# Weight sums of seven block pairs a layer, made between attention and retention and kept in HBM

## The chip, the cores and the metric

The kernel runs on one NeuronCore of a Trainium2 chip. The core has a matrix engine (TensorE, in the profile PE for the matmuls and PEld for the loads of their stationary operand), a vector engine (VectorE, DVE), a scalar engine (ScalarE, ACT), a general engine (GpSimd, POOL) and a queue engine (SyncE, SP). Each takes its own instructions in a fixed order, and they wait for each other through semaphores. SBUF is the memory on the core, PSUM holds what the matmuls accumulate, in banks of 128x512 float32, and HBM is the large memory outside, reached by DMA. A DMA is issued by SP, ACT or POOL. The metric is the device time of one execution in microseconds (us).

## The reference, cut to what matters

Two layers of the same form work on 512 tokens of width 1024, in float32:

```python
h = rmsnorm(x, g_mix)
z = h @ w_in                      # attention q k v, retention q k v, retention gate, gate_a, gate_b
ya = sliding_window_sink_attention(aq, ak, av, sinks) @ w_a
r = chunkwise_retention(rq, rk, rv)              # four heads
r = r * rsqrt(mean(r * r) + EPS) * silu(rg)      # per head
yb = r @ w_b                                     # 1024 x 1024
mixed = sigmoid(ga) * ya + sigmoid(gb) * yb
x = x + mixed @ w_out                            # 1024 x 1024
h2 = rmsnorm(x, g_mlp)
x = x + square(relu(h2 @ w_up)) @ w_down         # 1024 x 4096 and 4096 x 1024
```

A last rmsnorm follows the second layer. What the change touches is the weights of `w_b`, `w_out` and `w_up`.

## The kernel before, in words

Activations lie transposed in SBUF, channels on the partitions and the 512 tokens along them. Weights come from HBM in units of 128x1024 float32 (512 KB), in the order that `unit_order` writes down. Every weight and every activation is kept as a high and a low part, and a product is made of three matmuls, high by high, high by low and low by high (`products`, lines 295 to 303).

A unit goes through three steps. `load_until` (line 183) issues its DMA on SP into one of three `raw` tiles (line 195). `split_until` (line 230) makes the high part on ACT (line 255) and the low part on DVE (line 256); each of `hi` and `lo` has three tiles, so that the split of a unit waits until PE is done with the unit three before, and the load waits until the low part of the unit three before has been made. Then PE uses the unit. A plain unit holds PE for 24 matmuls of 512 columns.

Some products are made two blocks of 128 outputs at a time with fewer multiplications, by the scheme of Strassen and Winograd: the inner dimension is halved, the two blocks are the other half, and seven products of halves take the place of eight. The kernel calls this a pair. It needs sums of activations, made by `sum_input` and used as "forms", and sums of weights. With one = unit j and two = unit j+1, each cut into LEFT and RIGHT of 512 columns, a pair consists of four parts (`add_part`, lines 217 to 229, four DVE additions of 128x512):

- part 0: one.LEFT, and s1 = two.RIGHT + two.LEFT (line 221)
- part 1: s1 - one.LEFT (line 224), and one.RIGHT
- part 2: one.LEFT - two.RIGHT (line 228), and the right side of part 1 less its left side (line 229)
- part 3: two.LEFT alone

`load_part` (line 205) loads a pair with three DMAs: one.LEFT and the whole of two for part 0 (lines 210 and 212; two is also the tile of part 3), and one.RIGHT for part 1 (line 215). Parts 1 and 2 are tiles of another pool, `big`, which has seven tiles of 128x1024 and serves gates, sums, tables and other short-lived things. A part is split as a plain unit is. In `narrow_pair` (from line 580) the matmuls have 256 columns, so that PE is through with a part after 24 short matmuls; `wide_pair` takes high by high and high by low in one matmul of 512 columns and low by high in one of 256 (lines 1259 and 1260). Between the matmuls ACT copies partial results from bank to bank (lines 595, 598, 602), and DVE adds the rest into the outputs.

Each layer has, in order: the attention's q, k and v and the attention; gate_a, the first retention heads and half of the retention's gate; retention q and k of head 1 (`qk(1)`), the retention's values of the first two heads (`values(0)`), `w_a`, the retention of heads 0 and 1 beside `qk(2)`, `qk(3)` and `values(1)`; the rest of the retention beside the other gates; two pairs of `w_b` and four plain units; two plain units of `w_out` and three pairs; four plain units of `w_up` and then fourteen pairs of it, with the units of `w_down` in between. In the first layer `qk(1)` to `values(1)` runs from about 140 to 240 us, the pairs of `w_b` from 311, those of `w_out` from 372, and the first two of `w_up` from about 424 us.

Which instruction stands where on an engine is decided by a scheduler of the language before the run (`schedule_with_timeline_sim=True`), from a model of the times; on the chip the order on each engine is fixed. POOL does next to nothing: it clears a tile and sets a few constants, and it issues no DMA.

Of the kernel before, what the change touches and what calls it, by code (L numbers as in the profile page):

```python
# [11 lines left out]
F32 = mybir.dt.float32  # L12
F32R = mybir.dt.float32r
AF = mybir.ActivationFunctionType
ALU = mybir.AluOpType
# [3 lines left out]
P = 128  # L19
T = 512  # L20
# [30 lines left out]
ASIDE = 48  # L51
FIRST_WIDE, LAST_WIDE = 6, 32
BETWEEN = (0, 2, 4, 5)
H = T // 2
CROSSED = (0, 1, 4, 5, 2, 3, 6, 7)


def unit_order():

    def plain(name, *at):  # L60
        return [(name, i) for i in range(*at)]

    def pairs(src, *firsts):
        return [("pair", j, part, src) for j in firsts for part in range(4)]

    order = plain("w_in", 26) + plain("w_a", 4) + plain("w_in", 26, 46)
    order += pairs("w_b", 0, 2) + plain("w_b", 4, 8)
    order += plain("w_out", 2) + pairs("w_out", 2, 4, 6)
    for what, q, i in mlp_sequence():
        if what == "first":  # L70
            order += plain("w_up", 4)
        elif what == "pair":
            order += pairs("w_up", 8 * q + 2 * i)
        elif what == "down":
            order += plain("w_down", 8 * q + 2 * i, 8 * q + 2 * i + 2)
        else:
            order += plain("w_down", 8 * q, 8 * q + 8)
    return order
# [13 lines left out]
def wide(chunk):  # L92

    return FIRST_WIDE <= chunk < LAST_WIDE
# [32 lines left out]
def decoder(ctx, tc, xT, x_first, w_in, w_a, w_b, w_out, w_up, w_down, tables, decay, band, triangles, g_last, out):  # L127
    nc = tc.nc
    weights = {"w_in": w_in, "w_a": w_a, "w_b": w_b, "w_out": w_out, "w_up": w_up, "w_down": w_down}
# [5 lines left out]
    dram = ctx.enter_context(tc.tile_pool(name="dram", bufs=1, space=bass.MemoryType.DRAM))  # L135
# [6 lines left out]
    def temp(name="t"):  # L142
        return tmp.tile([P, T], F32, tag="t", name=name)

    def big(name, dtype=F32):
        return tmp.tile([P, 2, T], dtype, tag="big", name=name, bufs=7)
# [18 lines left out]
    order = [(layer, *u) for layer in range(DEPTH) for u in unit_order()]  # L165
    raws, parts, homes = {}, {}, []
    state = {"next": 0, "loaded": 0, "split": 0}

    def halves(i):

        return (slice(0, UNIT // 2), slice(UNIT // 2, UNIT)) if i < 3 else (slice(0, UNIT),)
# [3 lines left out]
    def raw_tile():  # L175
        return wpool.tile([P, UNIT], F32, tag="raw", name="raw")
# [25 lines left out]

    LEFT, RIGHT = slice(0, UNIT // 2), slice(UNIT // 2, UNIT)

    def load_part(i):
        layer, _, j, part, src = order[i]
        one, two = (weights[src][layer, j + a] for a in range(2))
        if part == 0:
            raws[i] = raw_tile()
            nc.sync.dma_start(raws[i][:, LEFT], one[:, LEFT])  # L210
            raws[i + 3] = raw_tile()
            nc.sync.dma_start(raws[i + 3], two)
        elif part == 1:
            raws[i] = big("raw2").rearrange("p a t -> p (a t)")
            nc.sync.dma_start(raws[i][:, RIGHT], one[:, RIGHT])

    def add_part(i):
        part = order[i][3]
# [12 lines left out]
    def split_until(n):  # L231
        while state["split"] < min(n, len(order)):
            i = state["split"]
            load_until(i + 3)
            paired = order[i][1] == "pair"
            if paired:
                add_part(i)
            raw = raws[i]
            if homes and i >= len(order) - len(homes):
                home = homes[len(order) - 1 - i]  # L240
                hi, lo = (home[:, 2 * a : 2 * a + 2, :].rearrange("p a t -> p (a t)") for a in range(2))
            else:


                first = (ASIDE, ASIDE) if paired else (0, 0)
                if paired and order[i][4] == "w_up" and wide(order[i][2]):
                    first = (ASIDE, 0)
                hi, lo = (
                    wpool.tile([P, UNIT + P], F32R, tag=n, name=n)[:, a : a + UNIT] for n, a in zip(("hi", "lo"), first)
                )  # L250
            for at in (LEFT,) if paired and order[i][3] == 3 else halves(i):
                if i == 0 and at.start == 0:
                    nc.vector.tensor_copy(hi[:, at], raw[:, at])
                else:
                    nc.scalar.activation(hi[:, at], raw[:, at], AF.Copy)  # L255
                last_low[:] = [nc.vector.tensor_tensor(lo[:, at], raw[:, at], f32(hi[:, at]), ALU.subtract).ins]  # L256
            raws.pop(i - 3 if paired else i, None)
            parts[i] = (hi, lo)
            state["split"] += 1

# [110 lines left out]
    def all_of(steps):  # L371
        for step in steps:
            step()
# [85 lines left out]
    def end(layer, uT):  # L459
# [32 lines left out]

        H = T // 2
        steps = [(b, at) for b in range(NB) for at in ((slice(0, T),) if b < NB - 1 else (slice(0, H), slice(H, T)))]

# [40 lines left out]
    def layer_body(layer):  # L536
# [6 lines left out]
        def forms_home():  # L543

            t = slots.four()
            form = t[0].rearrange("p a (b t) -> p (a b) t", t=H).rearrange("p (j k s) t -> p j k s t", k=2, s=2)
            return t, form

        def sum_input(by_form, b, ks):

            (b11, b12), (b21, b22) = ((t[:, :, :H], t[:, :, H:]) for t in b)
            f = [big("sums").rearrange("p a (b t) -> p (a b) t", t=H) for _ in range(2)]
            t1, t2, t3, t4 = f[0][:, 0:2, :], f[0][:, 2:4, :], f[1][:, 0:2, :], f[1][:, 2:4, :]
# [24 lines left out]
        def block(half, tokens):  # L578
            at = slice(tokens * H, tokens * H + H)
            return [x_homes[k // 2][0][:, k % 2 :: 2, at] for k in range(4 * half, 4 * half + 4)]  # L580
# [307 lines left out]
        def qk(h, rate=1.0):  # L888
            chunk("w_in", layer, xs, put_ret(rk, h), rate)
            chunk("w_in", layer, xs, put_ret(rq, h), rate)  # L890
# [3 lines left out]
        def values(pair):  # L894

            banks = [bank(ps_mm, "rv") for _ in range(NB)]
            for u in range(4):
                hi, lo = unit("w_in", layer)
                for j in range(2):
                    k = 2 * u + j  # L900
                    cols = slice(j * T, (j + 1) * T)
                    for b, ps in enumerate(banks):
                        at = slice(b * P, (b + 1) * P)
                        products(
                            ps, [(tuple(m[:, at] for m in xs[k]), (hi[:, cols], lo[:, cols]))], k == 0, k == KD - 1
                        )
                    advance()
            for b, ps in enumerate(banks):
                hi, lo = slots.one(), slots.one()
                split(view(hi), view(lo), ps, rcol[:, b : b + 1])  # L910
                rv[pair, b] = (hi, lo)
# [16 lines left out]
        def silu(i):  # L928
            s = temp("sig")
            nc.scalar.activation(s, rg[i], AF.Sigmoid)  # L930
            nc.vector.tensor_tensor(rg[i], rg[i], s, ALU.mult)
# [95 lines left out]
        def retention(pair):  # L1027
            two = [Head(2 * pair), Head(2 * pair + 1)]
            for head in two:
                for js in ((0, 1), (2, 3)):  # L1030
                    head.scores(js)
                    yield
            two[0].outputs(0)
            yield
            two[0].outputs(1)
            yield
            two[1].outputs(0)
            yield
            yield
            two[0].norm()  # L1040
            yield
            two[1].outputs(1)
            yield
            yield
            yield
            two[1].norm()
            yield
            yield
            while 4 * pair + 3 not in rg:
                yield  # L1050
            for head in two:
                head.finish()
                yield
            for i in (pair, pair + 2):
                homes_r[i] = forms_home()
                by_form_r[i] = homes_r[i][1]
            sum_input(by_form_r, [rg_tiles[2 * pair], rg_tiles[2 * pair + 1]], 2 * pair)
# [8 lines left out]
        with tc.issue_after(last_exp[0]):  # L1066
            for hs in (slice(0, T // 2), slice(T // 2, T)):
                nc.scalar.activation(x[:, :, hs], x[:, :, hs], AF.Sigmoid)
            for i in range(4):
                silu(i)  # L1070
        qk(1)

        values(0)


        aT = [(a_h[:, c, :], a_l[:, c, :]) for c in range(4)]
# [12 lines left out]
            slots.give(*t[1])  # L1089

        background.append(retention(0))
        qk(2)
        qk(3)
        values(1)
        drain()
        background.append(retention(1))
# [218 lines left out]
        def pair(q, i, late):  # L1315
# [5 lines left out]
            def step(ins):  # L1321
                now = next(turn)
                while late and now == BETWEEN[4 - len(late)]:
                    with tc.issue_after(ins), tc.issue_after(last_low[0]):
# [237 lines left out]
```

## Time and profile before

| | |
|---|---|
| median of 3 runs | 1479.65 us (1479.59 to 1479.96) |
| the profiled execution | 1481.1 us |
| its span, first to last instruction | 1478.5 us |
| PE busy | 1467.9 us, 99% of the span |
| PEld busy | 1249.9 us, 85% |
| DVE busy | 1162.7 us, 79% |
| ACT busy | 810.3 us, 55% |
| POOL busy | 3.8 us |
| HBM | 153.80 MB read, 8.40 MB written |
| granted clock of PE | 0.999 |

The profiled execution is 2.6 us longer than its span, and 1.45 us longer than the median of the runs. Busy time of PE counts a matmul from its start until its result is complete. Matmuls overlap, so that a 128x512 matmul lasts 390 ns while the next one starts 227 ns later; PE can therefore be busy while a matmul starts late, and only the starts, or the waits, tell of that. In the rows of a group the words after the bar are busy time, the mean of one in ns, and the idle time of that engine just before them with what ended it. In the waits, the columns are the total, the number of times and the longest.

### The profile page before, as it was taken

The page shows a single profiled execution, that of the slowest core. Times are in us where ns is not written, and L with a number is a line of the kernel's source. Part 1 is how long each engine was busy: PE and PEld are TensorE (multiplying, and loading weights), DVE is VectorE, ACT ScalarE, POOL GpSimd, SP SyncE. Part 2 cuts the span into 40 slices and gives each one's busy share as a digit, 9 for nine tenths or more (in the row PEclk, how much of TensorE's full clock was granted, in tenths as well). Part 3 has the DMA queues.
Part 4 walks back from the last instruction along what each step waited for, and adds up shares of the span by engine and source line. Part 5 has one row for each costly group of instructions (what it writes and reads, how often), then busy time and mean ns, then how long its engine had stood idle before and what let it go on. Part 6 is the DMA issues. An engine that isn't in the chain of part 4 may idle for free.

```text
span 1478.5 us, 20008 instructions
## 1 busy us (share of the span) xinstructions
PE 1467.9 (99%) x7466; PEld 1249.9 (85%) x7466; DVE 1162.7 (79%) x1920; ACT 810.3 (55%) x1302; POOL 3.8 (0%) x14
## 2 busy tenths in 40 slices
PE   9999999999999999999999999999999999999998
PEld 7888888888988888888888888888889888888887
DVE  7998668778998787776678975686889977878763
ACT  7656356654674445444556743656547654444553
POOL 0000000000000000000000000000000000000000
PEclk9999999999999999999999999999999999999999
DMA  6422223246323333333543232323553323333241
GB/s 226 135 87 86 93 82 104 93 164 191 102 79 114 100 114 94 106 100 115 170 128 91 85 98 89 99 92 98 175 167 104 101 97 99 115 101 112 89 141 57
DMA packets 56945, 166.13 MB, mean 112 GB/s; under 512 B 6896, under 2 KB 7056, under 8 KB 56848
## 3 DMA queue, kind: packets, MB, share of 16 engines
q1 hardware_dynamic: 56560, 164.33, 34.9%
q8 instruction: 58, 0.95, 0.3%
q10 hardware_dynamic: 288, 0.52, 0.1%
q14 instruction: 39, 0.32, 0.1%
HBM read 153.80 MB, written 8.40 MB: 110 GB/s over the span
## 4 chain that ended last, share of the span: by engine, by line
PE 86%; DVE 6%; issue 6%; DMA 1%; ACT 0%; POOLq 0%; DVEq 0%; SPq 0%
PE mm L303 20%; PE mm L301 20%; PE mm L302 20%; PE mm L1259 10%; PE mm L1260 5%; DVE lo L256 2%; PE rv L301 2%; PE rv L302 2%; PE rv L303 2%; DVE r L309 1%; PE score L797 1%; PE r L301 1%; PE r L303 1%; PE r L302 1%; DMA inv<-row 0%
## 5 line engine op out<-in xcount | busy, mean ns | idle before, releaser
L302 PE MATMUL mm<-r,hi 128*128 128x512 f32 (+1 forms) x1568 | 572.7, 367 | 0.0
L301 PE MATMUL mm<-r,hi 128*128 128x512 f32 (+1 forms) x1568 | 570.6, 368 | 1.4 <-ACT eu L598 0.7
L303 PE MATMUL mm<-r,lo 128*128 128x512 f32 (+1 forms) x1568 | 563.1, 367 | 1.6 <-DVE lo L256 1.3
L255 ACT ACTIVATE hi<-raw 128x1024 fp32r<-128x1024 f32 (+1 forms) x334 | 334.4, 1003 | 393.1 <-PE mm L302 210.9
L256 DVE TENSOR_TENSOR lo<-raw,hi 128x512 fp32r<-128x512 f32 (+1 forms) x335 | 385.2, 1152 | 118.8 <-ACT hi L255 115.7
L303 PEld LDWEIGHTS mm<-r,lo 128*128 128x128 f32 x1568 | 293.3, 188 | 51.1 <-DVE lo L256 3.7
L301 PEld LDWEIGHTS mm<-r,hi 128*128 128x128 f32 x1568 | 294.0, 188 | 50.2 <-ACT eu L598 1.5
L302 PEld LDWEIGHTS mm<-r,hi 128*128 128x128 f32 x1568 | 294.3, 188 | 45.7
L1259 PE MATMUL mm<-r,hi 128*128 128x512 f32 x728 | 251.9, 391 | 0.0
L1260 PE MATMUL mm<-r,lo 128*128 128x256 f32 x728 | 200.4, 277 | 1.2 <-DVE lo L256 1.1
L1259 PEld LDWEIGHTS mm<-r,hi 128*128 128x128 f32 x728 | 136.5, 188 | 28.3
L1260 PEld LDWEIGHTS mm<-r,lo 128*128 128x128 f32 x728 | 136.6, 188 | 5.2 <-DVE lo L256 2.7
L1339 DVE TENSOR_TENSOR x<-x,mm 128x512 f32<-128x512 f32 x56 | 37.8, 687 | 29.2 <-PE mm L303 29.2
L1332 ACT ACTIVATE z<-z 128x512 f32<-128x512 f32 x56 | 32.5, 624 | 48.3 <-DVE z L1312 48.3
L302 PE MATMUL rv<-lo,r 128*128 128x512 f32 x128 | 49.8, 389 | 0.0
L303 PE MATMUL rv<-hi,r 128*128 128x512 f32 x128 | 49.5, 389 | 0.0
L301 PE MATMUL rv<-hi,r 128*128 128x512 f32 x128 | 49.4, 390 | 0.0
L308 ACT ACTIVATE r<-z 128x512 fp32r<-128x512 f32 x64 | 38.7, 621 | 12.6 <-DVE z L1022 12.5
L309 DVE TENSOR_TENSOR r<-z,r 128x512 fp32r<-128x512 f32 x64 | 43.1, 686 | 2.8 <-ACT r L308 2.6
L824 ACT ACTIVATE sm<-sm,st 128x256 f32<-128x256 f32 (+1 forms) x64 | 30.2, 474 | 19.1 <-DVE st L812 18.9
L1312 DVE SCALAR_TENSOR_TENSOR z<-z,rstd 128x512 f32<-128x512 f32 x52 | 35.7, 687 | 0.6
L221 DVE TENSOR_TENSOR raw<-raw 128x512 f32<-128x512 f32 x38 | 26.0, 684 | 7.0 <-DMA raw<-w_up_in 6.3
(261 smaller groups left out, 1693.0 us busy)
## 6 DMA issues: line engine op xcount, KB each, us to landing
raw<-w_in_in SPq DMA_DIRECT2D x89, 512.0 KB, 3.6
raw<-w_down_in SPq DMA_DIRECT2D x64, 512.0 KB, 3.6
raw<-w_up_in SPq DMA_DIRECT2D x36, 512.0 KB, 3.6
raw<-w_up_in SPq DMA_DIRECT2D x56, 256.0 KB, 2.8
raw<-w_b_in SPq DMA_DIRECT2D x12, 512.0 KB, 4.0
raw<-w_out_in SPq DMA_DIRECT2D x10, 512.0 KB, 7.1
raw<-w_a_in SPq DMA_DIRECT2D x8, 512.0 KB, 3.5
aside<-gb SPq DMA_DIRECT2D x8, 512.0 KB, 4.7
```

Source lines behind the costliest of these rows:

```text
L255: nc.scalar.activation(hi[:, at], raw[:, at], AF.Copy)
L256: last_low[:] = [nc.vector.tensor_tensor(lo[:, at], raw[:, at], f32(hi[:, at]), ALU.subtract).ins]
L301: nc.tensor.matmul(ps, ah, bh, start=start and i == 0, stop=False, **more)
L302: nc.tensor.matmul(ps, ah, bl, start=False, stop=False, **more)
L303: nc.tensor.matmul(ps, al, bh, start=False, stop=stop and i == n - 1, **more)
L308: nc.scalar.activation(hi, src, AF.Copy)
L309: nc.vector.tensor_tensor(lo, src, f32(hi), ALU.subtract)
L1259: nc.tensor.matmul(both, hi[:, c], m, start=start and k == 0, stop=False, **more)
L1260: nc.tensor.matmul(ps[:, :H], lo[:, c], m[:, 0, :], start=False, stop=k == 3 and start, **more)
L1312: nc.vector.scalar_tensor_tensor(z[:, :, at], z[:, :, at], 0.0, factor, ALU.max, ALU.mult)
L1332: nc.scalar.activation(z[:, i, :], z[:, i, :], AF.Square)
L1339: nc.vector.tensor_tensor(x[:, c, :], x[:, c, :], ps, ALU.add)
```

## The change

Seven of the pairs of each layer, those that begin at units 0 and 2 of `w_b`, 2, 4 and 6 of `w_out` and 4 and 6 of `w_up`, get their four weight sums earlier. A new function `sums_ahead` loads the two units into two tiles of `big` by two DMAs issued on POOL, makes the four sums on DVE (one in a tile of the pool `t`, three in place), and stores them by four DMAs of 128x512, issued on POOL too, into a tensor in HBM. The calls of `sums_ahead` stand around `qk(1)`, `values(0)`, `qk(2)` and `qk(3)`: one, one, two, one, one and the last one, in the order of `PARKED`. When such a pair comes up, `load_part` loads each side of each part by a DMA of its own on SP, 128x512, from the weights or from the stored sums: seven DMAs for the pair in place of three, with all four parts in `raw` tiles, where before two parts were. `add_part` is left out for it, and a part's `raw` tile is given back after its own split.

```diff
+PARKED = (("w_b", 0), ("w_b", 2), ("w_out", 2), ("w_out", 4), ("w_out", 6), ("w_up", 4), ("w_up", 6))
...
+    park = {at: dram.tile([P, 4, T], F32, name="park_%s_%d" % at) for at in PARKED}
+
+    def is_parked(i):
+        return order[i][1] == "pair" and (order[i][4], order[i][2]) in park
+
     def load_part(i):
         layer, _, j, part, src = order[i]
         one, two = (weights[src][layer, j + a] for a in range(2))
+        if is_parked(i):
+            sums = park[src, j]
+            raws[i] = raw_tile()
+            sides = ((one[:, LEFT], sums[:, 0, :]), (sums[:, 1, :], one[:, RIGHT]), (sums[:, 2, :], sums[:, 3, :]), (two[:, LEFT],))
+            for side, part_of in zip((LEFT, RIGHT), sides[part]):
+                nc.sync.dma_start(raws[i][:, side], part_of)
+            return
         if part == 0:
...
+    def sums_ahead(layer, src, j):
+
+        w1, w2 = (big("ahead").rearrange("p a t -> p (a t)") for _ in range(2))
+        for a, w in enumerate((w1, w2)):
+            nc.gpsimd.dma_start(w, weights[src][layer, j + a])
+        s1 = temp("ahead1")
+        nc.vector.tensor_tensor(s1, w2[:, RIGHT], w2[:, LEFT], ALU.add)
+        nc.vector.tensor_tensor(w2[:, RIGHT], w1[:, LEFT], w2[:, RIGHT], ALU.subtract)
+        nc.vector.tensor_tensor(w1[:, LEFT], s1, w1[:, LEFT], ALU.subtract)
+        nc.vector.tensor_tensor(w1[:, RIGHT], w1[:, RIGHT], w1[:, LEFT], ALU.subtract)
+        for n, part in enumerate((s1, w1[:, LEFT], w2[:, RIGHT], w1[:, RIGHT])):
+            nc.gpsimd.dma_start(park[src, j][:, n, :], part)
...
-            if paired:
+            if paired and not is_parked(i):
                 add_part(i)
...
-            raws.pop(i - 3 if paired else i, None)
+            raws.pop(i - 3 if paired and not is_parked(i) else i, None)
...
+        to_park = [partial(sums_ahead, layer, *at) for at in PARKED]
+
+        def ahead(n):
+            all_of(to_park[:n])
+            del to_park[:n]
+
+        ahead(1)
         qk(1)
-
+        ahead(1)
         values(0)
+        ahead(2)
...
         background.append(retention(0))
+        ahead(1)
         qk(2)
+        ahead(1)
         qk(3)
+        ahead(9)
         values(1)
```

## The prediction

> **What bounds the kernel.** I read the page's first part, then the waits of the matrix engine, then stretches of time, then one stall in the timeline.
>
> ```profile
> span 1478.5 us, 20008 instructions
> PE 1467.9 (99%) x7466; PEld 1249.9 (85%) x7466; DVE 1162.7 (79%) x1920; ACT 810.3 (55%) x1302; POOL 3.8 (0%) x14
> ...
> PEld mm L303 <- DVE lo L256: 3.7, 6, 0.9
> PEld mm L1260 <- DVE lo L256: 2.7, 4, 0.8
> PEld mm L301 <- ACT eu L598: 1.5, 3, 0.6
> PEld mm L301 <- ACT eu L602: 0.9, 2, 0.5
> PEld mm L301 <- DVE gb L858: 0.3, 1, 0.3
> ```
>
> PE is the bound, and its number of matmuls isn't changed. All that the change can win is time in which PE waits. Those five rows are nearly all of it after the start: 3.7 + 2.7 + 1.5 + 0.9 + 0.3 = 9.1 us, of which 6.7 end with VectorE and 2.4 with ScalarE. The stretches show where (columns: the stretch and its length, busy time of PE, PEld, DVE, ACT and POOL with the number of instructions, clock, DMA share, GB/s):
>
> ```profile
> 140.00:190.00 50.00, 50.00 (x225) 41.54 (x224) 30.82 (x43) 20.73 (x29) 0.00 (x0) 1.00 0.31 100
> 190.00:230.00 40.00, 40.00 (x193) 33.88 (x192) 26.73 (x46) 23.55 (x38) 0.00 (x0) 1.00 0.30 87
> 311.00:345.00 34.00, 33.72 (x228) 30.77 (x227) 30.30 (x45) 19.25 (x28) 0.00 (x0) 1.00 0.63 202
> 345.00:372.00 27.00, 27.00 (x125) 22.47 (x124) 26.97 (x36) 12.69 (x16) 0.00 (x0) 1.00 0.60 195
> 372.00:404.00 32.00, 30.96 (x246) 29.77 (x245) 31.10 (x48) 21.17 (x35) 0.00 (x0) 1.00 0.30 90
> ...
> 431.00:450.00 19.00, 18.39 (x110) 15.63 (x109) 18.71 (x33) 13.73 (x22) 0.00 (x0) 1.00 0.36 113
> ```
>
> From 311 to 450 us DVE is busy 89 to 100%, and PE has its holes there, in the pairs of w_b, w_out and w_up. From 140 to 230 us DVE has 50 + 40 - 30.82 - 26.73 = 32.4 us to spare, and PE has no hole. One hole, in a w_out pair:
>
> ```profile
> 388.71 0.69 DVE raw L224
> 389.40 0.66 DVE r L312
> 390.06 0.33 DVE x L1199
> 390.39 0.60 DVE acc L395
> 390.99 1.15 DVE lo L256
> ...
> 391.23 0.28 PE L302 MATMUL mm<-r,hi 128*128 128x256 f32 x1
> 392.18 0.38 PE L303 MATMUL mm<-r,lo 128*128 128x256 f32 x1 [0.67 <-DVE lo L256]
> 392.40 0.28 PE L301 MATMUL mm<-r,hi 128*128 128x256 f32 x1
> ```
>
> The chain runs through DVE without a gap: a weight sum, work for the next norm, then the low part that PE waits for. PE starts these matmuls 0.12 us apart; here 0.95 passed, 0.83 too many.
>
> **The change, part by part.**
>
> *The sums leave the pairs.* Per pair four additions of 128x512:
>
> ```profile
> L221 DVE TENSOR_TENSOR raw<-raw x38: 627/692/694, 302.7 to 1406.7; 128x512 f32<-128x512 f32 x38
> ...
> L229 DVE TENSOR_TENSOR raw<-raw x38: 680/690/693, 321.3 to 1417.8; 128x512 f32<-128x512 f32 x38
> ...
> 328.48 0.68 DVE L228 TENSOR_TENSOR raw<-raw 128x512 f32<-128x512 f32 x1
> 329.08 0.69 DVE L229 TENSOR_TENSOR raw<-raw 128x512 f32<-128x512 f32 x1
> ```
>
> One lasts 0.69 us and the next starts 0.60 later, so a pair loses 4 x 0.60 = 2.4 us of DVE. The longest wait of PE for DVE is 0.9. In 311 to 345 us two pairs take 4.8 of 30.30 us off, in 372 to 404 three take 7.2 of 31.10, and the two of w_up give 4.8 before 450. The low parts come sooner by more than the waits, so I take 0.9 of the 6.7 us as won: 6.0. The upper bound is the whole 9.1, if ScalarE's copies come sooner too; the lower is 0, if what comes next is as late. Next in line are ScalarE's copies (line 598), for which PE waits until 378.1 us here:
>
> ```profile
> 376.56 0.71 ACT L311 ACTIVATE r<-x 128x512 fp32r<-128x512 f32 x1
> 377.17 0.61 ACT L394 ACTIVATE sq<-x 128x512 f32<-128x512 f32 x1
> 377.69 0.36 ACT L598 ACTIVATE eu<-mm 128x256 f32<-128x256 f32 x1
> ```
>
> ScalarE is held by work for the next norm, which no sum feeds. So the 2.4 us stay in the sum.
>
> *The sums come back earlier.* 7 x 2.4 = 16.8 us go into the 32.4 us that are free from 140 to 230 us; five pairs stand before about 190, where 12 us meet 19.2 free. By volume this costs nothing. By order it can: DVE takes instructions in turn, and a sum that waits for its load holds all behind it. The tightest place is the third pair. In the built order of DVE its first sum stands right after the low part that is made at 161.48 us, and ahead of the four instructions that empty the banks of the values:
>
> ```profile
> 161.48 1.23 DVE L256 TENSOR_TENSOR lo<-raw,hi 128x1024 fp32r<-128x1024 f32 x1 [2.85 <-ACT hi L255]
> 164.83 2.79 DVE L312 SCALAR_TENSOR_TENSOR r<-rv,rcol,r 128x512 fp32r<-128x512 f32 x4 [2.12 <-ACT r L311]
> ...
> 169.38 0.46 PE L301 MATMUL mm<-r,hi 128*128 128x512 f32 x1
> ...
> raw<-w_up_in SPq DMA_DIRECT2D x36, 512.0 KB, 3.6
> ...
> raw<-w_out_in SPq DMA_DIRECT2D x10, 512.0 KB, 7.1
> ...
> spill<-x SPq DMA_DIRECT2D x8, 256.0 KB, 2.0
> ```
>
> Its load reuses a tile of the first pair, and so waits on POOL for the first pair's last store. That sum ends about 155 us by the order, a store takes 2.0, a load 3.6, and POOL issues three more DMAs in between, for which I take an estimate of 1 us each, three times SP's 0.33. So the load is there at 155 + 1 + 2.0 + 2 + 3.6 = 163.6, against 162.7 when DVE comes to it. PE needs the first emptied bank at 169.38 less its 1 us of matmuls moved ahead: DVE can be late some 3 us. With 7.1 for the load, as in the DMA bursts, the 3.5 more just eat that. The traces show no DMA of POOL; between no cost and a late load at each of five pairs, I take 0.4 us a layer, nearer the free end because PE has three split units and a bank in hand.
>
> [...]
>
> *More loads on SP.* Seven DMAs in place of three a pair, at 0.33 us each to issue:
>
> ```profile
> raw<-w_up_in SPq DMA_DIRECT2D x56, 256.0 KB, 2.8
> ...
> raw<-w_out_in SPq DMA_DIRECT2D x12, 256.0 KB, 7.3
> ...
> L210 SPq DMA_DIRECT2D raw<-w_up_in x28: 327/328/328, 404.6 to 1399.6; - x28
> ...
> L256 DVE TENSOR_TENSOR lo<-raw,hi x335: 680/1221/1229, 6.0 to 1435.1; 128x1024 fp32r<-128x1024 f32 x127, 128x512 fp32r<-128x512 f32 x41
> L255 ACT ACTIVATE hi<-raw x334: 612/1062/1068, 6.9 to 1433.6; 128x1024 fp32r<-128x1024 f32 x164, 128x512 fp32r<-128x512 f32 x3
> ```
>
> 4 x 0.33 = 1.3 us more of SP a pair hide in the 9.9 us that PE takes for it (3.5 parts of 24 x 0.118, the pitch in the hole's rows). But the four parts now share three raw tiles, so a part's load waits for the low part of three parts before. The round is two issues 0.7, landing 2.8, high part 1.06, low part 1.22: 5.8 us, against 3 x 2.8 = 8.4 of PE. With the 7.3 of the burst it is 10.3 and 1.9 us late, of which a part's split can give back 2 x 2.8 - 2.3 = 3.3. That cover goes if DVE is still full, as from 345 to 372 us (26.97 of 27). Bounds 0 and 1.9 a layer; 0.35, since most of the burst lies before the pairs.
>
> *Traffic.* A layer adds 7 MB read and 7 MB written from 140 to 230 us, 163 GB/s on top of 87 to 100, and 5.5 MB in the pairs. PE loses 0.28 of 34 us through the 202 GB/s of 311 to 345 us, so I take it that only landings suffer; they are in the terms above. POOL's 42 issues a layer replace nothing, and only one clearing of a tile (late in the first layer) stands behind them.
>
> Sum against the profiled execution, 1481.1 us: -6.0 + 2 x 0.4 + 2 x 0.35 = -4.5, 1476.6. The median is 1.45 lower: 1475.2 us.
>
> **Rivals.**
>
> *DVE held by POOL's loads (slower).* Place: the first sum of the third to fifth pair, each with a load behind the stores of an earlier pair. If each of POOL's DMAs takes 3 us longer than assumed, a store and a load put the sum 6 us late; the bank's 3 us cover half, and 3 us of PE go per pair and layer: 3 x 3 x 2 = 18, less 6.0: +12, 1491.7. PE waits from 1.5 us a DMA on, and from 2 us the loss, 6 x (2 x 2 - 3) = 6, is more than the gain. For it: 163 on top of 100 GB/s is more than the 195 to 202 of the stretches where loads took 7 us. Against: PE has 50.00 of 50 us and 40.00 of 40 there, with slack that the trace doesn't use. [...]
>
> *The stalls change hands (no change).* DVE is early, but PE then waits for ScalarE's copies (2.4 us, kept) and for parts loaded late, 1.9 a layer: -6.0 + 3.8 + 0.8 = -1.4, 1478.2. For it: landings of 7 us in w_out. Against: the cover of 3.3 us.
>
> *All holes close.* -9.1, nothing lost: 1470.6. For it: ScalarE's copies often wait for tiles that DVE frees. Against: 378 us above.
>
> **How the numbers follow.** Forecast 0.52, all holes 0.06, change of hands 0.20, held DVE 0.22. Within 0.2% is 3.0 us either way, about what these runs can tell. Of the forecast's cases a tenth win less than 3.0: faster 0.53, same 0.25, slower 0.22. The likeliest case alone spans 1472.5 to 1477.5. The range leaves out a bit of the holes' end and the worse half of the held DVE: 1471 to 1486.
>
> **What would show it.** Right: lines 221 to 229 down from 38 to 24 each; DVE from 311 to 450 us lower by 16 us and higher by as much from 140 to 230; waits of the weight loads for line 256 below 1.5 us in total; no wait of PE from 140 to 270. Wrong: a DVE row of the new sums with several us of idle ended by a POOL DMA and PE waiting for line 312 or 1087 right after (held DVE); PE waiting for line 255 with a raw load as its last cause (change of hands).

## The result, and the profile after

| | before | after |
|---|---|---|
| median of the runs | 1479.62 us (4 runs, 1479.36 to 1479.96) | 1487.10 us (4 runs, 1485.48 to 1489.33) |
| the profiled execution | 1481.1 us | 1485.48 us, the fastest of the four |
| its span | 1478.5 us | 1483.7 us |

After over before is 1.0051, with a 95% interval of 1.0034 to 1.0069: 7.5 us slower, where 4.4 us faster was forecast. Lines 256, 301 to 303, 312, 595 and 598 of before are lines 282, 327 to 329, 338, 621 and 624 after; the four sums of a pair are now lines 247, 250, 254 and 255 where they stay in place, and 236 to 239 where they are made ahead. One execution of a kernel below, the five pairs with the copy first, took 1821 us at a clock of 0.75 and is left out of that kernel's ratio.

The page of the changed kernel begins with the busy time of each engine:

```profile
span 1483.7 us, 20353 instructions
...
PE 1468.5 (99%) x7466; PEld 1250.6 (84%) x7466; DVE 1162.6 (78%) x1920; ACT 810.1 (55%) x1302; POOL 49.4 (3%) x98
```

PE does the same work in nearly the same busy time, so the 5.2 us more of span are, for the most part, again time in which it waits or starts late. Counting the matmuls that start more than 0.15 us later than the usual pitch (0.227 us after a matmul of 512 columns, 0.118 after one of 256), PE lost 6.9 us before and 12.5 us after behind the start, in the two profiled runs. Its largest waits (total, times, longest):

```profile
PEld mm L327 <- ACT mm L621: 4.6, 3, 2.1
PEld mm L327 <- DVE r L338: 2.0, 1, 2.0
PEld mm L329 <- DVE lo L282: 1.8, 3, 1.0
PEld mm L327 <- DVE gb L884: 1.7, 2, 1.3
```

The waits that the change aimed at did go: those for low parts were 3.7 + 2.7 us, and of the first 1.8 us are left, of the second (line 1297 now) 0.4. New ones took their place: 4.6 for the first copy of a pair (line 621), which was in no row of before, 2.0 for the evacuation of the values' banks, 1.7 for the gates. The stretches, with the columns as in the prediction:

```profile
140.00:190.00 50.00, 48.42 (x216) 39.92 (x215) 36.78 (x54) 18.77 (x25) 14.03 (x26) 1.00 0.80 267
190.00:230.00 40.00, 40.00 (x193) 33.93 (x192) 34.91 (x62) 23.95 (x40) 7.06 (x13) 1.00 0.62 212
...
311.00:345.00 34.00, 31.60 (x205) 28.70 (x204) 26.74 (x38) 18.32 (x28) 0.00 (x0) 0.95 0.58 196
345.00:372.00 27.00, 27.00 (x126) 22.56 (x126) 23.24 (x31) 11.95 (x15) 0.00 (x0) 1.00 0.67 232
372.00:404.00 32.00, 30.96 (x237) 29.66 (x236) 26.52 (x38) 20.93 (x33) 0.00 (x0) 1.00 0.46 140
404.00:431.00 27.00, 27.00 (x142) 23.24 (x142) 22.87 (x30) 20.27 (x28) 0.00 (x0) 1.00 0.46 142
431.00:450.00 19.00, 18.95 (x135) 17.29 (x134) 17.79 (x25) 15.53 (x27) 0.00 (x0) 1.00 0.44 141
```

DVE does what was meant: 15.8 us less from 311 to 450 us, 14.1 more from 140 to 230. PE loses 1.6 us before 190 and 2.4 from 311 to 345, where its clock is 0.95 besides. I take the places one by one.

**At 171 us, in the first layer.** The chain of waits, in order of time (start, us, what):

```profile
156.46 5.57 DMA park_w_b<-ahead
162.31 6.98 DMA ahead<-w_out_in
169.32 0.70 DVE ahead L236
170.65 0.75 DVE r L338
```

A store of an earlier pair, then the third pair's load, then its first sum, and only then the first evacuation, for which PE starts 1.7 us late. DVE stood idle for 5.9 us ahead of that sum, and PE's reserve took up the rest. That is the place that the prediction named, with slower transfers. In the second layer the same sum waits 6.0 us at 899 us, and no matmul starts late for it. Over all pairs (KB each, median us to landing):

```profile
ahead<-w_out_in POOLq DMA_DIRECT2D x12, 512.0 KB, 6.8
park_w_out<-ahead POOLq DMA_DIRECT2D x24, 256.0 KB, 4.4
...
ahead<-w_b_in POOLq DMA_DIRECT2D x8, 512.0 KB, 4.7
park_w_b<-ahead POOLq DMA_DIRECT2D x16, 256.0 KB, 5.6
```

**At 320 us, the first pair of w_b.** The chain of waits there:

```profile
309.73 0.96 DVE own L447
310.71 1.58 DMA row<-own
312.30 3.76 DMA inv<-row
316.08 1.29 DVE z L1047 x2
317.38 1.22 DVE z L1048 x2
320.56 0.78 PE mm L327
```

This is the norm of the last retention head. Its reciprocal starts at 309.73 us; before it started 7.9 us sooner, as the timeline of before shows:

```profile
301.86 0.95 DVE L421 RECIPROCAL own<-own 128x128 f32<-128x128 f32 x1 [3.05 <-ACT own L420]
...
310.04 1.24 ACT L308 ACTIVATE r<-z 128x512 fp32r<-128x512 f32 x2 [1.33 <-DVE z L1022]
...
320.30 0.37 ACT L595 ACTIVATE mm<-mm 128x256 f32<-128x256 f32 x1
```

The timeline after, at the same place:

```profile
318.01 1.23 ACT L334 ACTIVATE r<-z 128x512 fp32r<-128x512 f32 x2 [1.48 <-DVE z L1048]
319.27 0.37 ACT L621 ACTIVATE mm<-mm 128x256 f32<-128x256 f32 x1
...
319.69 0.39 PE L327 MATMUL mm<-r,hi 128*128 128x256 f32 x1 [1.91 <-ACT mm L621]
```

ScalarE's queue now holds the splits of the retention's output ahead of the pair's first copy; they wait for the norm, the copy waits behind them, and PE behind the copy. Before, the norm was through 8 us sooner, and no matmul waited for it. PE then gets slower for a while (stretch, as above):

```profile
321.00:324.00 3.00, 3.00 (x8) 2.33 (x8) 3.00 (x6) 2.99 (x5) 0.00 (x0) 0.50 0.56 186
324.00:328.00 4.00, 4.00 (x20) 3.29 (x20) 3.03 (x6) 1.93 (x4) 0.00 (x0) 1.00 1.01 340
```

For 3 us after the wait the granted clock is 0.50, which is 1.5 us lost on top. In the second layer the same norm is late by less: 1.3 us at 1053 us.

The second layer has one more loss at 1076 us, with another cause. A matmul starts 0.7 us late for a high part (line 281) and one 0.7 us late for the low part after it. The chain of waits leads back to the load of that unit of w_b:

```profile
1069.54 4.96 DMA raw<-w_b_in
```

It is issued when its raw tile comes free, as the low part of an earlier part has been made, and lands 5.0 us later. So here a load comes late.

**At 382 and 1115 us, the first pair of w_out.** From the timeline:

```profile
379.58 0.71 ACT L337 ACTIVATE r<-x 128x512 fp32r<-128x512 f32 x1
380.20 0.62 ACT L417 ACTIVATE acc<-x 128x512 f32<-128x512 f32 x1
380.72 0.71 ACT L337 ACTIVATE r<-x 128x512 fp32r<-128x512 f32 x1
381.33 0.62 ACT L420 ACTIVATE sq<-x 128x512 f32<-128x512 f32 x1
381.85 0.36 ACT L621 ACTIVATE mm<-mm 128x256 f32<-128x256 f32 x1
...
382.27 0.39 PE L327 MATMUL mm<-r,hi 128*128 128x256 f32 x1 [1.04 <-ACT mm L621]
```

Four instructions for the next norm stand ahead of the copy, and PE starts 1.2 us late, once in each layer. Before, the built order had the copy first (at 372.60 us) and the norm's work from 375.42 on.

**Why the norm is late** isn't told by any duration. A scheduler writes the order of each engine before the run. In the order that PE is given, the sum of squares of the last retention head stands behind 927 matmuls of the products in the first layer before, and behind 951 after; in the second layer behind 4176 and 4186. Its matmul in the first layer, before:

```profile
299.91 0.39 PE L416 MATMUL ssq<-sh,ones 128*128 128x512 f32 x1
```

and after:

```profile
307.79 0.39 PE L442 MATMUL ssq<-sh,ones 128*128 128x512 f32 x1
```

At 0.227 us each, 24 matmuls are 5.4 us and 10 are 2.3; with the 1.7 us lost at 171 us, that makes 7.1 of the 7.9 us. So my theory was: **the sums made ahead change the built order, the norm goes behind, and the first w_b pair waits for it** (theory A below). The rival, theory B: the parts are loaded late, with seven loads in place of three and four parts in three raw tiles.

### The profile page after: what moved, and what is told of

It is laid out like the page before. It is cut to its first block, busy times and chain, and to the rows that moved or that the text cites. A ratio compares the mean times of both kernels' runs of the same rounds, so it can differ in the third digit from the quotient of the medians.

```text
span 1483.7 us, 20353 instructions
## 1 busy us (share of the span) xinstructions
PE 1468.5 (99%) x7466; PEld 1250.6 (84%) x7466; DVE 1162.6 (78%) x1920; ACT 810.1 (55%) x1302; POOL 49.4 (3%) x98
## 4 chain that ended last, share of the span: by engine, by line
PE 89%; issue 5%; DMA 3%; DVE 2%; ACT 1%; POOL 0%; POOLq 0%; ACTq 0%; DVEq 0%; SPq 0%
PE mm L327 21%; PE mm L329 21%; PE mm L328 21%; PE mm L1296 10%; PE mm L1297 5%; PE rv L327 2%; PE rv L328 2%; PE rv L329 2%; PE score L823 1%; DMA raw<-w_b_in 1%; DMA park_w_b<-ahead 1%; PE r L327 1%; PE r L329 1%; PE r L328 1%; PE pT L778 0%
## 5 line engine op out<-in xcount | busy, mean ns | idle before, releaser
L334 ACT ACTIVATE r<-sums 128x1024 fp32r<-128x1024 f32 x24 | 25.3, 1055 | 8.4 <-DVE sums L586 4.3
```

The source lines that it names most:

```text
L334: nc.scalar.activation(hi, src, AF.Copy)
```

## The experiments

All were timed beside the kernel before, which took 1479.64 to 1480.05 us in those sets.

### One side of the change at a time

Loads and pairs as in the changed kernel, without the sums:

```diff
-        to_park = [partial(sums_ahead, layer, *at) for at in PARKED]
+        to_park = []
...
-            sides = ((one[:, LEFT], sums[:, 0, :]), (sums[:, 1, :], one[:, RIGHT]), (sums[:, 2, :], sums[:, 3, :]), (two[:, LEFT],))
+            sides = ((one[:, LEFT], two[:, RIGHT]), (two[:, LEFT], one[:, RIGHT]), (one[:, LEFT], two[:, RIGHT]), (two[:, LEFT],))
```

> The sums are not made at all and nothing is stored; in the place of each stored sum the pair loads an unsummed side of the weights of the same size, so the seven products of these pairs are computed from wrong sums, and the loads of a pair, seven of 128x512 on SP, and the work of PE, ACT and DVE inside the pairs are as in the changed kernel. Theory A (the part made ahead does the harm: it puts the last two retention heads' norm behind, 24 matmuls in the first layer and 10 in the second in the built order, and that norm holds the first w_b pair): the norm stands where it stood before, the waits of PE at the start of the w_b pairs (2.07 + 0.31 us and the slow matmuls after them, 1.28 us) and the 1.74 us at 171 are gone, the waits of DVE stay gone; what is left is at most the copies of ScalarE at the w_out pairs, 2 x 1.3. Time 1479.6 - 6.0 + 2.6 = 1476 us, between 1474 and 1479. Theory B (the parts are loaded late: seven loads for three, three raw tiles for four parts): everything is lost that the changed kernel lost after 310 us, 1487.1 - 1.8 = 1485 us.

Measured 1476.96 us, ratio 0.9981 (0.9972 to 0.9990). Its largest wait (line numbers are one less than in the changed kernel):

```profile
PEld mm L326 <- ACT mm L620: 2.5, 2, 1.2
```

Theory B falls as the cause of the 7.5 us: with all 49 loads a layer in place, the pairs are faster than before. Of the new waits the copy in w_out is left; one for a later copy (line 623 of this kernel), at 325 us, is 0.9 us long. The late load at 1076 us is gone too. It is seen in the six kernels that make sums of w_b ahead and use them, so it takes both sides; why is not shown.

The other side, sums made and stored but not used:

```diff
-        return order[i][1] == "pair" and (order[i][4], order[i][2]) in park
+        return False
```

> The sums are loaded, made and stored ahead as in the changed kernel, but the pairs load their weights and make their sums as before, and nothing reads the stored ones. Theory A: all the losses of the part made ahead without the gain: 1.8 us at the third pair's sum, and the late norm at the w_b pairs, 4.2 us in the first layer with the slow matmuls and 1.4 in the second: 1479.6 + 7.4 = 1487 us, more if the sums inside the pairs now meet the late norm. Theory B: only the 1.8 us: 1481.4 us.

Measured 1493.63 us, ratio 1.0095 (1.0080 to 1.0111). The loss is all on this side, and larger than expected. Among its waits are

```profile
PEld mm L329 <- DVE lo L282: 6.5, 8, 1.6
PEld mm L327 <- ACT r L334: 3.5, 2, 2.4
...
PEld mm L1297 <- DVE lo L282: 2.7, 4, 0.8
```

The sums in the pairs now meet the late norm on DVE: low parts cost 6.5 + 2.7 us where before they cost 6.4 (and the bank at 171 costs 3.0, and the granted clock is 0.59 from 172 to 176 us and 0.66 from 322 to 327). So the two sides are not additive: -2.7 and +14.0 alone, +7.5 together.

### Is it the amount of added work, or its place?

Five pairs, those of w_out and w_up, same calls in the same places (five fill the calls up to the one between `qk(2)` and `qk(3)`):

```diff
-PARKED = (("w_b", 0), ("w_b", 2), ("w_out", 2), ("w_out", 4), ("w_out", 6), ("w_up", 4), ("w_up", 6))
+PARKED = (("w_out", 2), ("w_out", 4), ("w_out", 6), ("w_up", 4), ("w_up", 6))
```

> Only the three pairs of w_out and the two of w_up are made ahead, in the order of the same calls; the two of w_b are made in place as before. In the built order the retention's norms stand where they stood before the change (after 855, 927, 4107 and 4176 matmuls of the products), and the third pair's first sum still stands ahead of the evacuations. Theory A: no late norm, so the w_b pairs start as before; the waits of DVE in the w_out and w_up pairs close, 2.3 us a layer; 1.8 us stay at the third pair's sum, and 2 x 1.3 at ScalarE's copies: 1479.6 - 4.6 + 1.8 + 2.6 = 1479.4 us, and 1477 if the copies' order comes back too. Theory B: five of the seven pairs still load late, 1479.6 + 5/7 of 7.5 = 1485 us.

Measured 1481.42 us (1478.0 to 1484.3), ratio 1.0008 (1.0000 to 1.0017). The profiled run, the fastest, has no wait for the norm, 1.9 us at 171 and 1.2 + 1.2 at the copies. So the places are as theory A has them, and its 1479.4 is 2 us low. Across its runs the granted clock goes from 1.000 at 1478.0 us to 0.997 at 1484.3; a thousandth over 1480 us is 1.5 us.

The last call moved one projection later:

```diff
-        ahead(9)
         values(1)
         drain()
         background.append(retention(1))
+        ahead(9)
```

> The sums of the last two of the seven pairs, those of w_up, are called after the values of heads 2 and 3 instead of before them. In the built order the last retention norm then stands behind 984 matmuls of the products in the first layer and 4233 in the second: 33 and 47 later than in the changed kernel, at 0.227 us each 7.5 and 10.7 us. Theory A: the first w_b pair waits by that much longer, less what PE can do in between: 1487 + 18 = 1505 us, and no less than 1492. Theory B: as the changed kernel, 1487 us.

The expectation speaks of the last two pairs; at that point one is left, so that this moves one pair's sums only. Measured 1510.16 us, ratio 1.0206 (1.0192 to 1.0220): 23 us more than the changed kernel. The largest wait:

```profile
PEld mm L327 <- ACT r L334: 15.3, 4, 6.3
```

Four additions, called one projection later, cost three times the 7.5 us of the whole change. The amount of work is the same, so it can't explain that. The norm's place goes with it: 33 and 47 matmuls later than in the changed kernel.

The opposite: that last call left out, and all else as in the changed kernel.

```diff
-PARKED = (("w_b", 0), ("w_b", 2), ("w_out", 2), ("w_out", 4), ("w_out", 6), ("w_up", 4), ("w_up", 6))
+PARKED = (("w_b", 0), ("w_b", 2), ("w_out", 2), ("w_out", 4), ("w_out", 6), ("w_up", 4))
```

> The changed kernel without its last call, the one between the last two projections and the values of heads 2 and 3: that call makes the sums of one pair only, the second of w_up (the earlier run that moved that call moved one pair, not two). The other six pairs are called where the changed kernel calls them, and the second w_up pair makes its sums in place. In the built order the norms then stand behind 859, 927, 4111 and 4181 matmuls in place of 883, 951, 4115 and 4186. If one call of 2.4 us of VectorE at that place costs through the order: the 4.2 us at the first w_b pair go, and part of the 1.4 and 1.7 in the second layer; the wait at 171, the copies of w_out stay, and 0.5 a layer comes back in the second w_up pair: 1487.1 - 4.2 - 1.5 + 1.0 = 1482.4 us. If the cost goes by the amount of work ahead: six sevenths of it stay, 1486 us.

Measured 1482.81 us, ratio 1.0021 (1.0012 to 1.0030), against 1482.4 expected by the order and 1486 by the amount. The wait at the first w_b pair of the first layer is gone. That the sum came out so well is in part luck. In the profiled run, which at 1485.91 us is the second slowest of eleven, the second w_up pair costs 2.1 us in each layer where 0.5 was expected (the reason stands below, under fewer pairs), and the wait at 171 us is 2.8 us.

Over the kernels run, the place of the last norm in the built order goes with the late starts at the first w_b pair (how much later than the usual pitch PE starts a matmul that waits for the first copy, for the splits of the retention's output or for the gates, in the profiled run of each; some have more than one such start):

| kernel | calls right before `values(1)` | layer 1: behind, late | layer 2: behind, late |
|---|---|---|---|
| before | none, no sums made ahead | 927, 0 | 4176, 0.2 us |
| sums left out (e1), five pairs (e3, e8) | none | 927, 0 | 4176, 0 |
| two pairs (e10) | none | 917, 0 | 4176, 0 |
| three pairs (e9) | none | 917, 0 | 4181, 1.3 |
| four pairs (e12) | none | 927, 0 | 4181, 1.5 |
| six pairs (e11) | none | 927, 0 | 4181, 1.0 |
| seven pairs, calls spread (e6, e7) | none | 927, 0 | 4181, 1.0 and 1.2 |
| after | one | 951, 2.1 + 0.3 us | 4186, 1.3 |
| sums not used (e2) | one | 951, 2.4 + 0.4 | 4186, 1.0 + 0.6 |
| sums tied behind the evacuations (e5) | one | 951, 2.3 + 0.3 | 4186, 1.5 |
| last call later (e4) | none, one behind it | 984, 6.2 + 1.6 + 0.3 | 4233, 6.1 + 1.6 + 0.3 |

The kernels of this table that have not come up yet are told below.

### Can each wait be taken out?

The third and fourth sums are tied behind the evacuations on DVE:

```diff
         values(0)
-        ahead(2)
+        with tc.issue_after(last_bank[0]):
+            ahead(2)
```

> All seven pairs, called where the changed kernel calls them, but the sums of the third and fourth pair are tied behind the last evacuation of the values' banks on VectorE. The retention's norms stand in the built order as in the changed kernel (behind 883, 951, 4115 and 4186 matmuls of the products). If the harm is a sum of separate places, only the wait of 1.74 us at 171 us goes: 1487.1 - 1.8 = 1485.3 us, and 1483.7 if that wait also brought the slow matmuls of a lowered clock in most runs. If it is the amount of added work between 140 and 240 us: no change, 1487 us.

Measured 1487.84 us, ratio 1.0053 (1.0041 to 1.0066): nothing won. The wait at 171 is gone, but the timeline of DVE shows where it went:

```profile
194.89 0.69 DVE L236 TENSOR_TENSOR ahead<-ahead 128x512 f32<-128x512 f32 x1 [7.59 <-DMA ahead<-w_out_in]
195.50 1.48 DVE L1000 TENSOR_TENSOR s<-ret,dm 128x512 f32<-128x512 f32 x3
```

A later sum, held 7.6 us by its load, now stands ahead of the retention's masking, and PE starts a `ret` matmul 4.4 us late. This is rival one of the prediction, at another instruction.

Next the calls are spread so that none stands right before `values(1)`:

```diff
+        ahead(1)
         qk(0, PACE)
...
         values(0)
-        ahead(2)
+        with tc.issue_after(last_bank[0]):
+            ahead(1)
...
+        ahead(1)
         background.append(retention(0))
...
         qk(3)
-        ahead(9)
```

> As the run before, all seven pairs with the third behind the evacuations, but the calls are spread from one projection earlier: one before each of the first two, one behind the values, one behind w_a, one before and one behind the next projection, one more at the start, and none right before the values of heads 2 and 3. In the built order the norms stand behind 859, 927, 4111 and 4181 matmuls, as before the change or within 5. DVE does the same additions and POOL the same transfers. If the place of the norm is what costs, the waits at the start of the w_b pairs go, 4.2 + 1.4 us, and the late parts in the second layer with them: 1485.3 - 5.6 - 1.7 = 1478 us, near the 1477 of the run without the sums. If the amount of added work costs: 1485 us or more.

Measured 1484.70 us, ratio 1.0035 (1.0023 to 1.0048). The norm stands behind 927 and 4181 matmuls, and the wait at the first w_b pair of the first layer is gone, as in theory A; in the second layer 1.0 us stay. The 1478 us were missed because DVE is held elsewhere, ahead of the retention's masking (line 1000), by the first sum of a w_up pair: 4.6 us for its load at 191 us, and 6.4 at 923 in the second layer. The waits:

```profile
PEld ret L990 <- DVE s L1000: 3.9, 3, 2.3
PEld mm L327 <- ACT mm L621: 2.5, 2, 1.2
...
PEld mm L327 <- DVE gb L884: 1.1, 1, 1.1
```

Then the copies in w_out (with the seven pairs of the run above, and with five):

```diff
         def put_x(c):
...
-                next_input(c)
+                fresh_x.append(partial(next_input, c))
...
-            narrow_pair(pool, lambda ins: None, form_of(by_form_m), block_m, add_to_x(c))
+            narrow_pair(pool, after_copy, form_of(by_form_m), block_m, add_to_x(c))
```

`after_copy` issues the postponed work behind the first copy.

> As the run before, and in w_out the work for the next norm of the two plain units (four instructions on ScalarE) is tied behind the first copy between banks of the first pair, as the order had it before the change. The wait of 1.2 us for that copy goes in each layer: 2.4 us less than the run before, 1475.5 us. If ScalarE is simply late there, the wait moves to the next copy, and the time stays.

> Five pairs, those of w_out and w_up, with the third sum tied behind the evacuations and the norm's work behind the first copy; the pairs of w_b as before the change. Norms behind 855, 927, 4107 and 4176 matmuls, as before the change. From the profiled five pairs, 1478.0 us without a lowered clock: less 1.9 for the wait at 171 and 2.4 for the copies, 1473.7 us. That is 5.9 less than before the change; the late parts of the w_b pairs are the difference to the run with all seven, if they are worth anything.

Measured 1484.71 us, ratio 1.0025 (1.0015 to 1.0035), and 1481.03, 1.0006 (0.9997 to 1.0015). In both the row of line 621 is gone from the waits, so these 2.4 us of waits were the order on ScalarE. The time does not show it: with seven pairs it is 1484.71 us where the run before had 1484.70. Both miss their times because DVE is held by a sum's load again, now for longer (6.6 us in the run with five, and PE starts 3.5 us late at 195 us). In the run with seven:

```profile
PEld ret L990 <- DVE s L1000: 5.9, 3, 2.6
```

### Fewer pairs

The second pair of w_out and two of w_up; then the two of w_up alone; then three of w_out and the first of w_up, with the two ties:

```diff
+PARKED = (("w_out", 4), ("w_up", 4), ("w_up", 6))
...
+PARKED = (("w_up", 4), ("w_up", 6))
...
+PARKED = (("w_out", 2), ("w_out", 4), ("w_out", 6), ("w_up", 4))
```

> Three pairs alone, the second of w_out and the two of w_up, where PE waited longest for VectorE; their sums are made before and behind the first projection and behind the third. In the built order no sum stands ahead of the values' evacuations, the norms stand behind 860, 917, 4111 and 4181 matmuls, and ScalarE's first copy of w_out stands ahead of the next norm's work in the first layer as before. By the separate places: none of the new waits, and the four waits for low parts in these pairs go, 0.83 + 0.64 + 0.25 + 0.24 with the slow start after each some 2.2 a layer: 1479.7 - 4.4 = 1475.3 us. If the transfers or the added work on VectorE cost by their amount, 3/7 of the 7.5 us of the changed kernel comes on top: 1478.5 us.

> The two pairs of w_up alone, made before and behind the first projection. No load of POOL waits for a store of an earlier pair in a layer. The waits of 0.64 and 0.25 and the 0.24 behind them go, 1.3 us a layer: 1479.7 - 2.6 = 1477.1 us. By amount, 2/7 of 7.5 on top: 1479.2 us.

> Four pairs, the three of w_out and the first of w_up, with the third sum tied behind the values' evacuations, the fourth behind the projection after the next, and the next norm's work in w_out tied behind the first copy. Norms behind 859, 927, 4111 and 4181. Two pairs less go through POOL between 160 and 195 us than in the five-pair run where VectorE was held there for 3.5 us of PE. If the holds come from loads queued close together, none is left: the waits in w_out (1.8 a layer with the slow starts) and the first w_up pair (0.7) go, 1479.8 - 5.0 = 1474.8 us. If a sum behind the evacuations is held anyway, 2 to 3 us of it are lost again, 1477.5 us, no better than the two w_up pairs alone.

Measured 1480.87 us, ratio 1.0007 (0.9998 to 1.0016); 1477.57 us, 0.9981 (0.9972 to 0.9989); and 1481.73 us, 1.0011 (1.0002 to 1.0020). The two of w_up come within 0.5 us of their 1477.1 and are the fastest kernel here that leaves no work out, 0.19% faster than before. In part that is luck: of the 2.2 us by which late starts fell in its profile, 1.5 lie in w_up, where 2.6 were expected, and 0.7 at the first w_b pairs, where none were. The other two have no wait either where the sums are made, but they have two others. One is the norm in the second layer, behind 4181 matmuls, with 1.3 and 1.5 us. The other is new and stands behind a parked pair. The issues of SP in the run with four pairs, where the second w_up pair is made in place behind the first:

```profile
421.60 0.33 SPq L223 DMA_DIRECT2D raw<-w_up_in  x1
428.98 0.33 SPq L225 DMA_DIRECT2D raw<-w_up_in  x1
```

A pair made in place takes two raw tiles for its first part; behind a parked pair, whose parts hold all three, the second load is issued 7.4 us after the first. It lands at 432.7 us, the sum and the high part follow, PE loses 2.1 us in each layer, and the largest wait is

```profile
PEld mm L1303 <- ACT hi L281: 2.8, 2, 1.4
```

In the run with three pairs the same happens to the third pair of w_out: 1.1 us late in the first layer, 2.1 in the second. I had not expected it.

## Why the prediction was wrong, step by step

- *All that the change can win is PE's waits, 6.0 of 6.7 us.* Right in kind: waits for low parts fell from 6.4 to 2.2 us, lines 221 to 229 from 38 to 24 rows each, DVE by 15.8 us from 311 to 450. The size was too high for low parts alone: the 6.7 us are waits of the weight loads, and the matmuls behind the low parts started 4.5 us late in all. The run without the sums won 2.7 us net of 2.4 of late starts for the first copies: about 5, with the later copies (lines 598 and 602) coming sooner too.
- *"The sums come back earlier. By volume this costs nothing. By order it can."* **This is the step that failed**, with its 0.4 us a layer, 0.8 us in all. I looked at one order, that of DVE, and at one place in it. The orders of PE and ScalarE came out otherwise too when work was added. With one call right before the values of heads 2 and 3, a norm of the first layer stands 24 matmuls later, and PE lost 2.1 + 0.3 us and some 1.5 of slow clock at the first pair of w_b. In the second layer that norm stands 10 later, 5 of them with this call, and PE lost 1.3 us, of which 1.0 stay without it. No term of the sum stood for that. Leaving the call out gave 4.3 us back, from 1487.10 to 1482.81, net of the 2.1 us a layer that its own pair then cost in place. Why the scheduler answers a call at that place in this way was not looked into.
- *The tightest place, the third pair.* Right in place: the first sum, ahead of the evacuations. The load was put at 163.6 us and landed at 169.3. The mis-sized terms are the store, 2.0 taken and 4.4 to 5.6 found, and the load, 3.6 taken and 7.0 found there; the issue on POOL, 1 us taken, was 0.54. The reserve was nearer 4 than 3 us: DVE was held for 5.9, and PE lost 1.7, in the first layer alone.
- *Next in line are ScalarE's copies, line 598.* The engine was right, and so was the reason, work for the next norm on ScalarE. The instruction was not: the built order now has that work ahead of the first copy (line 595 of before), 1.2 us in each layer. Tied back, the wait goes. That the scheduler does this because DVE is free earlier in its model is my guess, not shown.
- *More loads on SP, 0.35 a layer.* The run without the sums shows no wait for a late part, so the round of three tiles has room enough by itself. The changed kernel paid 1.4 us in the second layer and nothing in the first, against 0.7 in the sum: there a load took 5.0 us to land, where the round was worked out with 2.8. It is a cost, too, where a pair in place follows a parked one.
- *The rivals.* "DVE held" has the right place and the right cause, and shows in its pure form where the sums were moved (4.4 us at 196); it is 1.7 of the 5.2 us of span. "Stalls change hands" is the w_out copy and, once, a high part with a late raw load behind it (1076 us). The largest loss, at the first w_b pair, was in neither.
- *The signs.* Of those named for "right", the rows of lines 221 to 229 and DVE's busy time came as said. Waits for low parts were to be below 1.5 us and were 2.2, and PE was not to wait from 140 to 270 us and waited at 171. Those named for "wrong" both showed, the first with PE waiting for line 312 (now 338).
- *The median.* The prediction took it 1.45 us below the profiled execution. After, it is 1.6 above it: the profiled run is the fastest of four, and the others show a clock of 0.997 and 0.996 where it shows 0.998. Together that is 3.1 of the 11.9 us between forecast and result.

## What to carry to other kernels

Where a scheduler writes the order, compare the built orders of every engine before costing anything: find the critical producers (here a norm) and count how many instructions of the busy engine stand ahead of them in each. Work moved into idle time isn't free if it waits for a transfer on an engine that takes instructions in turn (here DVE stood idle for 5.9 us ahead of one sum); it needs its load landed, with room for a slow landing (here 7.0 us, where 3.6 had been taken). Move few items at a time, and look at what follows each: here two of the seven pairs won 2.5 us, and three, four or five won nothing.

## What the runs showed of the hardware

A wait of PE cost more than its length here. After a matmul that started 2.1 us late, at 319.69 us, the clock was 0.50 from 321 to 324 us, 1.5 us more. The same is seen in the profiled run of the six pairs, behind a wait of 2.8 us at 171:

```profile
172.50:175.50 3.00, 3.00 (x9) 2.35 (x8) 3.00 (x6) 0.00 (x0) 1.23 (x3) 0.50 0.49 182
```

Not each such wait is followed by it. In the five-pair run with the copy first, the stretch behind a wait of 3.5 us:

```profile
195.00:199.00 4.00, 3.62 (x17) 3.12 (x18) 4.00 (x8) 3.56 (x7) 1.08 (x2) 1.00 0.34 131
```

In the seven-pair run with the copy first, a wait of 2.4 us at 194 was followed by a mean clock of 0.59 from 193.7 to 197.7 us, and one of 2.2 at 926 by a clock of 1.00 from 926.5 to 930. What decides which of these waits is followed by the lower clock was not shown; their length alone doesn't, as 2.1 us was followed by it and 3.5 was not. That the half clock is what spreads the runs of the changed kernel over 4 us is argued from their clocks, 0.998 in the fastest and 0.996 in the slowest, not shown: one execution of each was profiled.

The clock doesn't explain every spread: the run without the sums lay between 1474.83 and 1478.33 us at clocks of 0.999 and 1.000. What varies there stays open.

POOL's transfers took 0.54 us each to issue in the median, beside a DVE that is 74 to 87% busy, and 2.9 to 6.8 us to land in the median of their kinds. The loads for w_b and w_out took 4.7 and 6.8 us, and the stores 5.6 and 4.4, with 212 to 267 GB/s moving in all; the prediction had taken 3.6 and 2.0 from SP's transfers of the same sizes.
